# Opening stage of a two-layer block: modulation rows and the sum of squares moved to TensorE

## The chip, the cores and the metric

One core of one Trainium2 chip runs the whole kernel as one program. The metric is device time in microseconds (us), the median of several runs. Engines: TensorE (PE in the profile; PEld is its weight load), VectorE (DVE), ScalarE (ACT), GpSimd (POOL), SyncE (SP, which here only issues DMAs).

## The reference, cut to what matters

The whole is one block on T = 256 tokens of D = 1024 features (attention mixers, a feed-forward part, an expert lookup). The change touches only its first lines: the vector `c` makes six modulation vectors; the first two, shift and scale, act on the normalised input; the result goes into the wide input projection.

```python
def rmsnorm(x, g):
    return x * lax.rsqrt(jnp.mean(x * x, axis=-1) + 1e-6) * g

mod = silu(c) @ w_ada + b_ada              # 6*D values; shift = mod[:D], scale = mod[D:2*D], ...
h = rmsnorm(x, norm1_g) * (1 + scale) + shift
z = h @ w_in                               # w_in: D x 5704, cut into tiles of 128 columns
```

## The kernel before, in words

Features lie on the partitions: `x` is 8 feature tiles of 128 features by 256 tokens. All products keep fp32 accuracy by a split into a high and a low part of a rounded type (fp32r): a product is three matmuls, high by high, high by low, low by high. A weight tile (128 x 1024, 512 KB) is loaded by SyncE into `wraw`, ScalarE rounds it to the high part (L98), and DVE or GpSimd subtracts to get the low part (L100).

The opening stage (`first_mixer`) does this:

- SyncE loads `c` as a row and `x` in four pairs of feature tiles. PE spreads `c` over 128 partitions (L251), ScalarE makes `cond` = silu(c) of it.
- ScalarE squares `x` in pairs (L303); DVE adds the pairs down to one tile (L305 to L307); one fp32 matmul with a matrix of ones sums it over the partitions (L314). DVE takes the mean (L326) and the reciprocal root (L172 to L174, with ScalarE's logarithm and exponential between) into `rstd`.
- `xr` = `x` * `rstd`: the first pair of feature tiles on DVE, the other three pairs on GpSimd (L336).
- For each feature tile k two rows of `w_ada` are needed, row 8+k (scale) and row k (shift). A row is a tile of 128 x 1024 values, loaded by SyncE into one of four buffers (two for even k, two for odd k), and DVE multiplies it by `cond` and sums along each partition in one instruction (L266), which gives one column of `mod`. Then DVE adds `b_ada` (L270), makes `gs` (L389), ScalarE makes the normalised tile `hn` high (L393) and `y`, and DVE the low part of `hn` (L395).
- PE multiplies the `hn` tiles by nine block tiles of `w_in` (256 columns for each matmul, L361 and L363) and by four tiles for the value projection (512 columns). A matmul is issued when both its feature tile and its weight tile are known.

The order of all this is written out by hand in the string `ORDER`: "a" takes the next feature tile (rows, `mod`, `gs`, `hn`, and the matmuls with the weight tiles there so far), "w" the next block tile, "v" the next tile of the value projection. `LOWS` says for each of the 13 weight tiles whether DVE ("v") or GpSimd ("g") makes the low part. All engines work through their own instructions in program order. The first matmul of the step after the stage is that of L469.

Of the kernel before, what the change touches and what calls it, by code (L numbers as in the profile page):

```python
# [9 lines left out]
FT = mybir.dt.float32  # L10
# [3 lines left out]
AF = mybir.ActivationFunctionType  # L14
OP = mybir.AluOpType
# [4 lines left out]
T = 256  # L20
D = 1024
KT = 8
EPS = 1e-6
NEG = -3.0e38
TAKEN = -3.4e38
ORDER = "wwawaavavwwawavwwaawv"
LOWS = "vgvgvgvvvvvgv"
EXP_LN = 6
SILU = 18
PLAN = "ijjaavaasvqvqvksskkssksqssrgrqsssrgss0gr1rggr0rrrgrg1rg20g31rg2rrg3rrgg23rg"  # L30
# [40 lines left out]
class Net:  # L71
# [171 lines left out]
    def load_cond(self, pool):  # L243

        nc = self.nc
        row = pool.tile([1, D], FT, name="crow")
        nc.sync.dma_start(row, self.ap["c"])
        self.cond = pool.tile([128, D], FT, name="cond")
        pss = [self.ps([128, 512], "mm") for _ in range(2)]
        for z, ps in enumerate(pss):  # L250
            nc.tensor.matmul(ps, self.ones[0:1, :], row[:, 512 * z:512 * z + 512], start=True, stop=True)  # L251

        def finish():
            for z, ps in enumerate(pss):
                self.last_act = nc.scalar.activation(self.cond[:, 512 * z:512 * z + 512], ps, AF.Silu)
            self.condd = self.dram.tile([1, D], FT, name="condd")
            nc.scalar.dma_start(self.condd, self.cond[0:1, :])
        return finish
# [25 lines left out]
    def first_mixer(self):  # L284
        nc, tc, ap = self.nc, self.tc, self.ap
        with ExitStack() as es:
            x1 = es.enter_context(tc.tile_pool(name="x1", bufs=1, side="right"))
            x = self.x = x1.tile([128, KT, T], FT, name="x")
            P = es.enter_context(tc.tile_pool(name="m1", bufs=1))
            A = es.enter_context(tc.tile_pool(name="m1a", bufs=1))  # L290
# [5 lines left out]
            nc.vector.tensor_scalar(self.upper, self.relx[:, 128:], 0.0, None, op0=OP.is_gt)  # L296
            self.table = self.act_table(SILU)
            cond = self.load_cond(A)
            sq = P.tile([128, KT, T], FT, name="sqs", tag="bias1")
            for k in range(0, KT, 2):  # L300
                nc.sync.dma_start(x[:, k:k + 2], ap["x"][:, k:k + 2])
                with tc.issue_after(self.table):
                    high = nc.scalar.activation(sq[:, k:k + 2], x[:, k:k + 2], AF.Square)  # L303
                if k % 4:
                    nc.vector.tensor_add(sq[:, k - 2:k], sq[:, k - 2:k], sq[:, k:k + 2])  # L305
            nc.vector.tensor_add(sq[:, :2], sq[:, :2], sq[:, 4:6])
            pair = nc.vector.tensor_add(sq[:, 0], sq[:, 0], sq[:, 1])  # L307
            with tc.issue_after(high.ins):
                cond()
            self.table = self.act_table(EXP_LN, self.last_act)  # L310
            nc.scalar.dma_start(self.vecs, self.ap["vecs"])
            nc.scalar.dma_start(self.b_ada, self.ap["b_ada"])
            ps = self.ps([128, T], "sm")
            nc.tensor.matmul(ps, self.ones, sq[:, 0], start=True, stop=True)  # L314
            r = P.tile([128, T], FT, name="rstd")
            n1 = Scratch(P.tile([128, 3 * T], FT, name="norm1", tag="kx"))
            ms = n1.tile([128, T], FT, name="ms")
            rows = [Scratch(P.tile([128, 2 * D], FT, name=f"ada{i}", tag=t)) for i, t in enumerate(("sgb", "bias1"))]

            def ada_row(k, j):  # L320
                self.ada_one(A, j, rows[k % 2].tile([128, D], FT, name="ada", bufs=2))

            with tc.issue_after(pair.ins):
                ada_row(0, 8)
            with tc.issue_after(self.last_ada.ins):
                mean = nc.vector.tensor_scalar(ms, ps, 1.0 / D, EPS, op0=OP.mult, op1=OP.add)  # L326
            with tc.issue_after(mean.ins):
                ada_row(0, 0)
            with tc.issue_after(self.last_ada.ins):
                self.rsqrt(n1, r, ms, [128, T])  # L330
            norm_exp = self.last_exp
            bg = P.tile([128, KT], FT, name="bg")
            nc.vector.scalar_tensor_tensor(bg, self.b_ada[:, 8:16], 1.0, self.vecs[:, 0], op0=OP.add, op1=OP.mult)
            xr = P.tile([128, KT, T], FT, name="xr", tag="sga")
            for k in range(0, KT, 2):
                (nc.gpsimd if k else nc.vector).tensor_tensor(  # L336
                    xr[:, k:k + 2], x[:, k:k + 2], r[:, None, :].to_broadcast([128, 2, T]), op=OP.mult)

            hn = self.hi_lo("hn0")
            qi = P.tile([128, 4, T], FT, name="qi", tag="qx")  # L340
# [3 lines left out]
            first, parts, lows, heads = [], [], [], {}  # L344
            known = 0
            F = tc.tile_pool(name="m1f", bufs=1)
            f = F.__enter__()
# [4 lines left out]
            spare += [[f.tile([128, D], FR, name=f"w0{i}{j}") for j in range(2)] for i in range(3)]  # L352
            banks = [self.ps([128, 2, T], t) for t in ("acc", "acc", "mm", "mm", "sm")]
            vacc = [self.ps([128, 512], "acc") for _ in range(2)]
            nlow = iter(LOWS)

            def product(bank, out, l, r, last):

# [6 lines left out]
            def block_part(i, k, a, b):  # L365
                o = slice(k * 128, k * 128 + 128)
                product(i // 2, banks[i // 2][:, i % 2], first[i][a][:, o], hn[b][:, k], a == 1 and k == KT - 1)

            def v_part(c, a, b):
                for k in (2 * c, 2 * c + 1):  # L370
                    for tb in range(2):
                        product(8 + tb, vacc[tb], hn[b][:, k, tb * 128:tb * 128 + 128],
                                parts[c][a][:, (k % 2) * 512:(k % 2) * 512 + 512], a == 1 and k == KT - 1)

            def later(part, *a):
                lows.append(lambda: part(*a))

            def flush():
                while lows:
                    lows.pop(0)()  # L380

            for e in ORDER:
                if e == "a":
                    k = known
                    if k:
                        ada_row(k, 8 + k)
                        ada_row(k, k)
                    self.ada_end(k, k + 1)
                    nc.vector.scalar_tensor_tensor(self.gs[:, 0, k:k + 1], self.mod[:, 8 + k:9 + k],  # L389
                                                   self.vecs[:, 0, k:k + 1], bg[:, k:k + 1], op0=OP.mult, op1=OP.add)  # L390
                    y = P.tile([128, T], FT, name="y1", bufs=2)
                    for t in (hn[0][:, k], y):
                        nc.scalar.activation(t, xr[:, k], AF.Identity, scale=self.gs[:, 0, k:k + 1],  # L393
                                             bias=self.mod[:, k:k + 1])
                    nc.vector.tensor_tensor(hn[1][:, k], y, hn[0][:, k].bitcast(FT), op=OP.subtract)  # L395
                    flush()
                    for b in range(2):
                        for i in range(len(first)):
                            block_part(i, k, 0, b)
                    for i in range(len(first)):  # L400
                        block_part(i, k, 1, 0)
                    known += 1
                    continue
                c = len(parts)
                with tc.issue_after(norm_exp.ins), tc.issue_after(self.last_rsqrt.ins):
                    w = self.weights(ap["w_in"][len(first) if e == "w" else 9 + c], next(nlow),
                                     spare.pop() if e == "w" else None)
                if e == "w":
                    i = len(first)
                    first.append(w)  # L410
                    flush()
                    for k in range(known):
                        block_part(i, k, 0, 0)
                        block_part(i, k, 0, 1)
                        later(block_part, i, k, 1, 0)
                else:
                    parts.append(w)
                    flush()
                    v_part(c, 0, 0)
                    v_part(c, 0, 1)  # L420
                    later(v_part, c, 1, 0)
# [4 lines left out]
            ps = banks[4][:, 0]  # L426
# [40 lines left out]
            ps = self.ps([128, 2, 8], "sm")  # L467
# [4 lines left out]
            with tc.issue_after(qi_last.ins):  # L472
# [4 lines left out]
                ps = self.ps([128, 384], "sm")  # L477
# [5 lines left out]
                rows = self.dram.tile([128, 8 * 384], FT, name="rows")[:, :]  # L483
                nc.scalar.dma_start(rows, bass.AP(tensor=line.tensor, offset=line.offset, ap=[[0, 128], [1, 8 * 384]]))
                bias = []
                for tb in range(2):
# [3 lines left out]
                                                   ap=[[8 * 384 - 1, 128], [384, 8], [1, n]]))  # L490
# [70 lines left out]
            for j2 in range(4):  # L561
                wa = self.weights(ap["w_proj"][2 * j2])
                wb = self.weights(ap["w_proj"][2 * j2 + 1])
                for i in range(2):
                    j = 2 * j2 + i
                    pa = self.fm_block(wa, ya, 4, i * 512, self.ps([128, T], "acc"))
                    m = W.tile([128, T], FT, name="m")
# [16 lines left out]
            for j in range(8):  # L584
                ps = self.fm_block(self.weights(ap["w_out"][j]), mg)
                nc.vector.scalar_tensor_tensor(x[:, j], ps, self.mod[:, 16 + j:17 + j], x[:, j],
                                               op0=OP.mult, op1=OP.add)
# [851 lines left out]
def _col(v):  # L1439
    return v.reshape(-1, 128).T  # L1440
# [10 lines left out]
def prepare(inputs):  # L1451
    i = {k: np.asarray(v) for k, v in inputs.items()}
    ar = np.arange
    o = {}
    o["x"] = i["x"][0].T.reshape(8, 128, 256).transpose(1, 0, 2)
    o["mem"] = i["mem_2"][0].T.reshape(8, 128, 256).transpose(1, 0, 2)
    o["c"] = i["c"]
    o["w_ada"] = i["w_ada"][0].T.reshape(48, 128, 1024)
    o["b_ada"] = _col(i["b_ada"][0])
    o["vecs"] = np.stack([_col(v) for v in (  # L1460
        i["norm1_g"][0], i["norm2_g"][0], i["final_g"], i["norm_mix_g_2"][0], i["norm_xattn_g_2"][0],
        i["norm_mem_g_2"][0], i["norm_ffn_g_2"][0])], axis=1)
    w = i["w_in"][0]
# [14 lines left out]
    w = i["w_in_2"][0]  # L1478
# [39 lines left out]
```

## Time and profile before

| what | us |
|---|---|
| median of 3 runs (lowest, highest) | 1450.46 (1448.54, 1452.81) |
| the profiled execution's own time | 1451.56 |
| its span in the profile | 1449.8 |
| PE busy in the span | 1382.8 (95%) |
| DVE busy | 1102.9 (76%) |
| ACT busy | 756.3 (52%) |
| POOL busy | 151.3 (10%) |

The span is what the profile shows; the time of the execution holds 1.76 us more around it. A row of a timeline reads: start and length in us, engine, line of the kernel, operation, written tile <- read tiles, shape, count of instructions put together, and in brackets how long the engine had been idle and what ended that.

### The profile page before, as it was taken

Reading aid. Unit: us, or ns where it says so; the run is one execution under the profiler, and the core shown is the slowest. Engines: PE = TensorE matmul, PEld = TensorE weight load, DVE = VectorE, ACT = ScalarE, POOL = GpSimd, SP = SyncE. Lnnn points to the kernel's source line nnn. Section 1 sums busy time; section 2 is a strip of 40 time slices with the busy share of each in tenths; the row PEclk is TensorE's granted clock in tenths of the full one; section 3 lists DMA queues with packets and bytes.
Section 4 is the critical chain, followed back from the end, with each engine's and each line's share of the span. In section 5 each row is a group of like instructions: output and inputs, shape, how many; then the busy total and the mean of one; then the engine's idle time right before and its main releaser. Section 6 shows DMA issues by size and latency. Waiting matters only on the chain. (4 is left out here: it accounts for less than half of the span.)

```text
span 1449.8 us, 28871 instructions
## 1 busy us (share of the span) xinstructions
PE 1382.8 (95%) x11584; PEld 1326.8 (92%) x11584; DVE 1102.9 (76%) x2082; ACT 756.3 (52%) x1358; POOL 151.3 (10%) x64
## 2 busy tenths in 40 slices
PE   4989899999898999999999999999999999899997
PEld 2879799899898999999999999999999879799996
DVE  7797988549999888999856556665557796777776
ACT  4546664455445555555554444444445465655555
POOL 3100000018995000000000000000000000000001
PEclk9999999999999999999999999999999999999998
DMA  7766776655555545545566666776664444266662
GB/s 278 268 202 230 267 243 200 207 186 156 169 186 161 168 153 166 166 151 171 152 207 221 198 189 192 240 233 201 186 188 141 148 123 157 74 189 191 192 193 94
DMA packets 76234, 269.51 MB, mean 186 GB/s; under 512 B 8970, under 2 KB 11202, under 8 KB 75460
## 3 DMA queue, kind: packets, MB, share of 16 engines
q1 hardware_dynamic: 71426, 257.99, 55.6%
q10 hardware_dynamic: 4674, 9.69, 2.0%
q8 instruction: 90, 1.47, 0.4%
q14 instruction: 44, 0.36, 0.1%
HBM read 265.01 MB, written 4.21 MB: 186 GB/s over the span
## 5 line engine op out<-in xcount | busy, mean ns | idle before, releaser
L98 ACT ACTIVATE wh<-wraw 128x1024 fp32r<-128x1024 f32 x431 | 456.3, 1061 | 522.8 <-PE ps_acc L130 244.1
L100 DVE TENSOR_TENSOR wl<-wraw,wh 128x1024 fp32r<-128x1024 f32 x384 | 470.3, 1227 | 253.9 <-ACT wh L98 251.1
L129 PE MATMUL ps_acc<-c,wh 128*128 128x256 f32 x1024 | 286.6, 280 | 0.0
L130 PE MATMUL ps_acc<-c,wh 128*128 128x256 f32 x1024 | 286.5, 280 | 0.0
L131 PE MATMUL ps_acc<-c,wl 128*128 128x256 f32 x1024 | 286.5, 280 | 0.0
L131 PE MATMUL ps_mm<-hn,wl 128*128 128x256 f32 x680 | 190.1, 280 | 9.8 <-DVE wl L100 7.1
L131 PE MATMUL ps_acc<-hn,wl 128*128 128x256 f32 x696 | 192.5, 277 | 4.7 <-POOL wl L100 4.7
L129 PE MATMUL ps_mm<-hn,wh 128*128 128x256 f32 x680 | 192.6, 283 | 2.7 <-ACT wh L98 2.6
L129 PE MATMUL ps_acc<-hn,wh 128*128 128x256 f32 x696 | 193.9, 280 | 0.0
L129 PEld LDWEIGHTS ps_acc<-c,wh 128*128 128x128 f32 x1024 | 192.5, 188 | 0.1
L131 PEld LDWEIGHTS ps_acc<-c,wl 128*128 128x128 f32 x1024 | 192.5, 188 | 0.0
L130 PEld LDWEIGHTS ps_acc<-c,wh 128*128 128x128 f32 x1024 | 192.5, 188 | 0.0
L130 PE MATMUL ps_acc<-hn,wh 128*128 128x256 f32 x696 | 192.4, 277 | 0.0
L130 PE MATMUL ps_mm<-hn,wh 128*128 128x256 f32 x680 | 189.5, 279 | 0.0
L131 PEld LDWEIGHTS ps_mm<-hn,wl 128*128 128x128 f32 x680 | 128.2, 189 | 11.6 <-DVE wl L100 8.6
L100 POOL TENSOR_TENSOR wl<-wraw,wh 128x1024 fp32r<-128x1024 f32 x47 | 131.8, 2826 | 56.4 <-ACT wh L98 56.2
L131 PEld LDWEIGHTS ps_acc<-hn,wl 128*128 128x128 f32 x696 | 130.8, 188 | 5.4 <-POOL wl L100 5.4
L129 PEld LDWEIGHTS ps_mm<-hn,wh 128*128 128x128 f32 x680 | 128.9, 190 | 5.2 <-ACT wh L98 3.3
L130 PEld LDWEIGHTS ps_acc<-hn,wh 128*128 128x128 f32 x696 | 130.7, 188 | 0.2 <-DVE hn L281 0.2
L129 PEld LDWEIGHTS ps_acc<-hn,wh 128*128 128x128 f32 x696 | 130.4, 188 | 0.4 <-ACT hn L280 0.2
L130 PEld LDWEIGHTS ps_mm<-hn,wh 128*128 128x128 f32 x680 | 128.5, 189 | 0.2
L1404 POOL TENSOR_TENSOR big<-big 128x512 f32<-128x512 f32 x4 | 5.0, 1265 | 981.8 <-DVE big L1401 981.8
(484 smaller groups left out, 2770.9 us busy)
## 6 DMA issues: line engine op xcount, KB each, us to landing
wraw<-in_peer_u_dram SPq DMA_DIRECT2D x128, 512.0 KB, 4.0
wraw<-in_peer_v_dram SPq DMA_DIRECT2D x128, 512.0 KB, 4.4
wraw<-in_w_in_dram SPq DMA_DIRECT2D x70, 512.0 KB, 4.8
wraw<-in_ffn_up_dram SPq DMA_DIRECT2D x44, 512.0 KB, 3.6
wraw<-in_ffn_down_dram SPq DMA_DIRECT2D x22, 512.0 KB, 3.6
ada<-in_w_ada_dram SPq DMA_DIRECT2D x16, 512.0 KB, 6.0
wraw<-in_w_out_dram SPq DMA_DIRECT2D x16, 512.0 KB, 4.6
wraw<-in_peer_wq_dram SPq DMA_DIRECT2D x16, 512.0 KB, 3.6
```

Of the source, the lines that this page charges most:

```text
L98: nc.scalar.activation(h, raw, AF.Copy)
L100: (nc.vector if eng == "v" else nc.gpsimd).tensor_tensor(l, raw, h.bitcast(FT), op=OP.subtract)
L129: mm(out, a[0], b[0], start=first, stop=False, **kw)
L130: mm(out, a[0], b[1], start=False, stop=False, **kw)
L131: self.last_mm = mm(out, a[1], b[0], start=False, stop=last, **kw)
L1404: nc.gpsimd.tensor_tensor(xf[:, tb, cs], xt[:, tb, cs], fg[:, cs], op=OP.mult)
```

## The change: rows on TensorE, sum of squares on TensorE, another order

The two rows of each of the first `ADA_PE` = 4 feature tiles are no longer multiplied on DVE. Each row is stored transposed in blocks of 128, and PE multiplies its eight blocks (128 x 128, the stationary operand, fp32) by one column of `cond_col` each, eight matmuls summed into one column of `mods`. `cond_col` is silu of the new input `c_col`, `c` with features on the partitions. `mods` lies in the PSUM bank that takes the sum of squares. That sum is now eight matmuls with ones, one for each feature tile; the four adds on DVE are gone. GpSimd does nothing in the stage: all low parts and all pairs of `xr` are DVE's, and a pair of `xr` is made when the first of its tiles comes up. `crow` is loaded from ScalarE's queue, `ccol` is the first load on SyncE's. The string `ORDER` is another one. Feature tiles 4 to 7 keep their rows on DVE.

```diff
-ORDER = "wwawaavavwwawavwwaawv"
-LOWS = "vgvgvgvvvvvgv"
+ORDER = "awwawawawwvvaawwvwaav"
+ADA_PE = 4
...
-        nc.sync.dma_start(row, self.ap["c"])
+        nc.scalar.dma_start(row, self.ap["c"])
+        col = pool.tile([128, KT], FT, name="ccol")
+        nc.sync.dma_start(col, self.ap["c_col"])
+        self.cond_col = pool.tile([128, KT], FT, name="cond_col")
+        with self.tc.issue_after(self.table):
+            nc.scalar.activation(self.cond_col, col, AF.Silu)
...
+            ps = self.ps([128, 2 * T], "sm")
+            mods = ps[:, T:T + 16]
+            def ada_row(k, j):
+                w = rows[k % 2].tile([128, D], FT, name="ada", bufs=2)
+                if k >= ADA_PE:
+                    return self.ada_one(A, j, w)
+                self.load(w, self.ap["w_ada"][j])
+                for i in range(KT):
+                    with tc.issue_after(bank.ins):
+                        nc.tensor.matmul(mods[:, j:j + 1], w[:, i * 128:i * 128 + 128], self.cond_col[:, i:i + 1],
+                                         start=False, stop=i == KT - 1, skip_group_check=True)
...
-                if k % 4:
-                    nc.vector.tensor_add(sq[:, k - 2:k], sq[:, k - 2:k], sq[:, k:k + 2])
-            nc.vector.tensor_add(sq[:, :2], sq[:, :2], sq[:, 4:6])
-            pair = nc.vector.tensor_add(sq[:, 0], sq[:, 0], sq[:, 1])
+                for i in (k, k + 1):
+                    with tc.issue_after(bank.ins) if i else ExitStack():
+                        m = nc.tensor.matmul(ps[:, :T], self.ones, sq[:, i], start=i == 0, stop=i == KT - 1,
+                                             skip_group_check=True)
+                    bank = bank if i else m
...
-            nc.tensor.matmul(ps, self.ones, sq[:, 0], start=True, stop=True)
...
-            with tc.issue_after(pair.ins):
-                ada_row(0, 8)
-            with tc.issue_after(self.last_ada.ins):
-                mean = nc.vector.tensor_scalar(ms, ps, 1.0 / D, EPS, op0=OP.mult, op1=OP.add)
+            mean = nc.vector.tensor_scalar(ms, ps[:, :T], 1.0 / D, EPS, op0=OP.mult, op1=OP.add)
+            ada_row(0, 8)
+            ada_row(0, 0)
             with tc.issue_after(mean.ins):
-                ada_row(0, 0)
-            with tc.issue_after(self.last_ada.ins):
                 self.rsqrt(n1, r, ms, [128, T])
...
-            for k in range(0, KT, 2):
-                (nc.gpsimd if k else nc.vector).tensor_tensor(
-                    xr[:, k:k + 2], x[:, k:k + 2], r[:, None, :].to_broadcast([128, 2, T]), op=OP.mult)
+            def scaled(k):
+                nc.vector.tensor_tensor(xr[:, k:k + 2], x[:, k:k + 2], r[:, None, :].to_broadcast([128, 2, T]),
+                                        op=OP.mult)
...
-                    self.ada_end(k, k + 1)
-                    nc.vector.scalar_tensor_tensor(self.gs[:, 0, k:k + 1], self.mod[:, 8 + k:9 + k],
+                    if k % 2 == 0:
+                        scaled(k)
+                    on_pe = k < ADA_PE
+                    raw = mods if on_pe else self.mod
+                    nc.vector.tensor_add(self.mod[:, k:k + 1], raw[:, k:k + 1], self.b_ada[:, k:k + 1])
+                    nc.vector.scalar_tensor_tensor(self.gs[:, 0, k:k + 1], raw[:, 8 + k:9 + k],
```

On PE the stage began like this before: the spread of `c`, the one sum, then block matmuls of feature tile 0 with the first two weight tiles (`hn_153` is the high part of `hn`, `hn_154` the low part, `w_...` parts of block tiles).

```order
L251 MATMUL ps_mm<-crow,ones 128x512 x2
L314 MATMUL ps_sm<-sqs,ones 128x256
L363 MATMUL ps_acc<-hn_153,w_176 128x256
L361 MATMUL ps_acc<-hn_153,w_174 128x256
L363 MATMUL ps_acc<-hn_153,w_172 128x256
```

Now the start of PE's program reads so (`ada_112` is the buffer of feature tile 0's rows, `ada_113` that of tile 1's):

```order
L325 MATMUL ps_sm<-sqs,ones 128x256
L256 MATMUL ps_mm<-crow,ones 128x512 x2
L325 MATMUL ps_sm<-sqs,ones 128x256 x7
L315 MATMUL ps_sm<-cond_col,ada_112 128x1 x16
L315 MATMUL ps_sm<-cond_col,ada_113 128x1 x16
L374 MATMUL ps_acc<-hn_168,w_191 128x256
L372 MATMUL ps_acc<-hn_169,w_191 128x256
```

The four rows of tiles 0 and 1 stand ahead of the first block matmul. The rows of tile 2 stand further on in PE's program, with three block matmuls between them (high part of `hn`, three weight tiles):

```order
L315 MATMUL ps_sm<-cond_col,ada_112 128x1 x8
L372 MATMUL ps_acc<-hn_168,w_191 128x256
L372 MATMUL ps_acc<-hn_168,w_189 128x256
L372 MATMUL ps_acc<-hn_168,w_187 128x256
L315 MATMUL ps_sm<-cond_col,ada_112 128x1 x8
L372 MATMUL ps_acc<-hn_169,w_191 128x256
```

On DVE, before, tile 0's rows stood around the mean (`norm_131`) and the steps of the reciprocal root:

```order
L266 SCALAR_TENSOR_TENSOR junk,mod<-ada_132,cond 128x1024
L389 SCALAR_TENSOR_TENSOR gs<-mod,vecs,bg 128x1
L326 TENSOR_SCALAR norm_131<-ps_sm 128x256
L266 SCALAR_TENSOR_TENSOR junk,mod<-ada_132,cond 128x1024
L172 TENSOR_TENSOR norm_131<-norm_131 128x256
L270 TENSOR_TENSOR mod<-mod,b_ada 128x1
L173 SCALAR_TENSOR_TENSOR norm_131<-norm_131 128x256
L174 SCALAR_TENSOR_TENSOR rstd<-norm_131 128x256
L100 TENSOR_TENSOR w_177<-wraw,w_176 128x1024
L336 TENSOR_TENSOR xr<-x,rstd 128x512
```

Now the same place on DVE has no row; `mod` and `gs` read the PSUM bank, and the reciprocal root stands behind them:

```order
L337 TENSOR_SCALAR norm_140<-ps_sm 128x256
L403 TENSOR_TENSOR mod<-ps_sm,b_ada 128x1
L404 SCALAR_TENSOR_TENSOR gs<-ps_sm,vecs,bg 128x1
L172 TENSOR_TENSOR norm_140<-norm_140 128x256
L173 SCALAR_TENSOR_TENSOR norm_140<-norm_140 128x256
L174 SCALAR_TENSOR_TENSOR rstd<-norm_140 128x256
L100 TENSOR_TENSOR w_192<-wraw,w_191 128x1024
L348 TENSOR_TENSOR xr<-x,rstd 128x512
```

So DVE's chain to the first `xr` now waits for two rows on PE where it had two rows of its own.

## Rows read from the trace of the kernel before

**Rows 1.** The page, busy time of each engine, share of the span, instructions.

```profile
PE 1382.8 (95%) x11584; PEld 1326.8 (92%) x11584; DVE 1102.9 (76%) x2082; ACT 756.3 (52%) x1358; POOL 151.3 (10%) x64
```

**Rows 2.** Stretches: length, busy PE, PEld, DVE, ACT, POOL, PEclk, DMA share, GB/s.

```profile
10.00:20.00 10.00, 2.23 (x5) 1.22 (x5) 9.89 (x16) 5.30 (x8) 5.12 (x3) 1.00 0.96 363
20.00:30.00 10.00, 5.34 (x18) 4.26 (x18) 9.95 (x13) 2.04 (x3) 5.29 (x3) 1.00 0.45 138
...
34.80:68.70 33.90, 32.99 (x236) 30.63 (x234) 25.92 (x38) 19.40 (x28) 4.90 (x2) 1.00 0.78 281
```

**Rows 3.** Waits, 0 to 34.8 us: total, times, longest.

```profile
ACT hn L393 <- DVE mod L270: 12.3, 3, 7.3
```

**Rows 4.** Timeline: marks of the stage, on ACT and PE.

```profile
17.64 0.60 ACT L393 ACTIVATE hn<-xr,mod,gs 128x256 fp32r<-128x256 f32 x1 [1.50 <-DVE xr L336]
18.29 0.58 PE L363 MATMUL ps_acc<-hn,w 128*128 128x256 f32 x1 [6.35 <-ACT hn L393]
...
34.18 0.60 ACT L393 ACTIVATE hn<-xr,mod,gs 128x256 fp32r<-128x256 f32 x1 [1.97 <-DVE mod L270]
...
68.72 0.29 PE L469 MATMUL ps_sm<-ident,wiT 8*128 8x8 f32 x2
```

**Rows 5.** Groups by line and form, 0 to 70 us: busy, mean ns, idle before.

```profile
L266 DVE SCALAR_TENSOR_TENSOR junk<-ada,cond 128x1024 f32<-128x1024 f32 x16 | 21.7, 1354 | 0.1
...
L305 DVE TENSOR_TENSOR sqs<-sqs 128x512 f32<-128x512 f32 x2 | 1.4, 693 | 3.1 <-ACT sqs L303 3.1
```

**Rows 6.** Timeline, 14 to 33 us: DVE, and one GpSimd instruction.

```profile
14.72 1.22 DVE L100 TENSOR_TENSOR w<-wraw,w 128x1024 fp32r<-128x1024 f32 x1
15.86 1.75 DVE L336 TENSOR_TENSOR xr<-x,rstd 128x512 f32<-128x512 f32 x1
...
20.90 2.53 POOL L100 TENSOR_TENSOR w<-wraw,w 128x1024 fp32r<-128x1024 f32 x1
21.14 3.37 DVE L266 SCALAR_TENSOR_TENSOR junk<-ada,cond 128x1024 f32<-128x1024 f32 x1
...
28.64 2.32 DVE L389 SCALAR_TENSOR_TENSOR gs<-mod,vecs,bg 128x1 f32<-128x1 f32 x1
...
32.59 0.21 DVE L389 SCALAR_TENSOR_TENSOR gs<-mod,vecs,bg 128x1 f32<-128x1 f32 x1
```

**Rows 7.** Timeline of PE: block matmuls of 256 columns.

```profile
18.67 0.41 PE L361 MATMUL ps_acc<-hn,w 128*128 128x256 f32 x1
18.89 0.41 PE L363 MATMUL ps_acc<-hn,w 128*128 128x256 f32 x1
...
31.78 1.01 PE L361 MATMUL ps_acc<-hn,w 128*128 128x256 f32 x3 [1.22 <-ACT hn L393]
...
58.31 0.52 PE L361 MATMUL ps_acc<-hn,w 128*128 128x256 f32 x3
```

**Rows 8.** PE with narrow matmuls: timeline, durations (lowest, median, highest ns), stretches.

```profile
195.41 1.40 PE L188 MATMUL ps_sm<-ones,sq 128*128 128x1 f32 x12
...
1100.26 2.06 PE L188 MATMUL ps_sm<-big 128*128 128x2 f32 x9
...
L188 PE MATMUL ps_sm<-big x11: 251/352/352, 1100.0 to 1102.0; 128*128 128x2 f32 x11
...
195.41:196.81 1.40, 1.40 (x15) 1.40 (x14) 1.40 (x4) 1.27 (x3) 0.00 (x0) 1.00 0.80 269
1100.20:1102.10 1.90, 1.90 (x11) 1.90 (x10) 1.44 (x2) 0.32 (x1) 0.00 (x0) 0.50 0.85 246
```

**Rows 9.** Timeline, 0 to 12 us: the spread of `c`, a Square, the mean.

```profile
2.49 3.75 PE L251 MATMUL ps_mm<-crow,ones 1*128 1x512 f32 x4 [2.49 <-DMA crow<-in_c_dram]
4.11 0.63 ACT L303 ACTIVATE sqs<-x 128x512 f32<-128x512 f32 x1 [2.10 <-DMA x<-in_x_dram]
...
11.98 0.42 DVE L326 TENSOR_SCALAR norm<-ps_sm 128x256 f32<-128x256 f32 x1
...
L251 PE MATMUL ps_mm<-crow,ones 1*128 1x512 f32 x4 | 3.7, 1089 | 2.5 <-DMA crow<-in_c_dram 2.5
```

**Rows 10.** The page, DMA issues of the rows: KB each, us to landing.

```profile
ada<-in_w_ada_dram SPq DMA_DIRECT2D x16, 512.0 KB, 6.0
```

More of the change, by code (lines that the diff above doesn't have):

```diff
@@ L298, in first_mixer @@
             cond = self.load_cond(A)
-            sq = P.tile([128, KT, T], FT, name="sqs", tag="bias1")
+            rows = [Scratch(P.tile([128, 2 * D], FT, name=f"ada{i}", tag=t)) for i, t in enumerate(("sgb", "bias1"))]
+            ps = self.ps([128, 2 * T], "sm")
[9 more added lines that the diff above has]
+                                         start=False, stop=i == KT - 1, skip_group_check=True)
+            sq = P.tile([128, KT, T], FT, name="sqs", tag="hm1")
             for k in range(0, KT, 2):
@@ L303, in first_mixer @@
                     high = nc.scalar.activation(sq[:, k:k + 2], x[:, k:k + 2], AF.Square)
-                if k % 4:
-                    nc.vector.tensor_add(sq[:, k - 2:k], sq[:, k - 2:k], sq[:, k:k + 2])
-            nc.vector.tensor_add(sq[:, :2], sq[:, :2], sq[:, 4:6])
-            pair = nc.vector.tensor_add(sq[:, 0], sq[:, 0], sq[:, 1])
-            with tc.issue_after(high.ins):
-                cond()
+                for i in (k, k + 1):
[3 more added lines that the diff above has]
+                    bank = bank if i else m
+                if k == 4:
+                    with tc.issue_after(high.ins):
+                        cond()
             self.table = self.act_table(EXP_LN, self.last_act)
@@ L312, in first_mixer @@
             nc.scalar.dma_start(self.b_ada, self.ap["b_ada"])
-            ps = self.ps([128, T], "sm")
-            nc.tensor.matmul(ps, self.ones, sq[:, 0], start=True, stop=True)
             r = P.tile([128, T], FT, name="rstd")
@@ L317, in first_mixer @@
             ms = n1.tile([128, T], FT, name="ms")
-            rows = [Scratch(P.tile([128, 2 * D], FT, name=f"ada{i}", tag=t)) for i, t in enumerate(("sgb", "bias1"))]
-            def ada_row(k, j):
-                self.ada_one(A, j, rows[k % 2].tile([128, D], FT, name="ada", bufs=2))
-            with tc.issue_after(pair.ins):
-                ada_row(0, 8)
-            with tc.issue_after(self.last_ada.ins):
-                mean = nc.vector.tensor_scalar(ms, ps, 1.0 / D, EPS, op0=OP.mult, op1=OP.add)
+            mean = nc.vector.tensor_scalar(ms, ps[:, :T], 1.0 / D, EPS, op0=OP.mult, op1=OP.add)
+            ada_row(0, 8)
+            ada_row(0, 0)
             with tc.issue_after(mean.ins):
-                ada_row(0, 0)
-            with tc.issue_after(self.last_ada.ins):
                 self.rsqrt(n1, r, ms, [128, T])
@@ L354, in first_mixer @@
             vacc = [self.ps([128, 512], "acc") for _ in range(2)]
-            nlow = iter(LOWS)
             def product(bank, out, l, r, last):
@@ L405, in first_mixer @@
                 with tc.issue_after(norm_exp.ins), tc.issue_after(self.last_rsqrt.ins):
-                    w = self.weights(ap["w_in"][len(first) if e == "w" else 9 + c], next(nlow),
+                    w = self.weights(ap["w_in"][len(first) if e == "w" else 9 + c], "v",
                                      spare.pop() if e == "w" else None)
@@ L1457, in prepare @@
     o["c"] = i["c"]
+    o["c_col"] = _col(i["c"][0])
     o["w_ada"] = i["w_ada"][0].T.reshape(48, 128, 1024)
+    pe = [j + k for j in (0, 8) for k in range(ADA_PE)]
+    o["w_ada"][pe] = o["w_ada"][pe].reshape(-1, 128, 8, 128).transpose(0, 3, 2, 1).reshape(-1, 128, 1024)
     o["b_ada"] = _col(i["b_ada"][0])
```

## The prediction

> **What bounds the kernel now.** I read the totals first: TensorE (PE) is busy for 95% of the span [rows 1], so a time lost or won in the opening lasts to the end unless PE later stands still for other reasons. The table by stretch says where PE is not the limit [rows 2]: between 10 and 30 us it works 7.6 us of 20 while VectorE (DVE) works 19.8. From 34.8 to 68.7 PE is busy 32.99 of 33.90 us. Up to 34.8 us the opening is therefore bound by whatever makes the normalised feature tiles, behind that by PE. The waits say the same: ScalarE's `hn` waits 12.3 us for `mod` on DVE [rows 3], and PE for `hn`. So the mark that carries the result is when the fourth feature tile's `hn` is there: 34.18 + 0.60 = 34.78 us [rows 4]. Behind it stand 33.9 us of PE work up to the first matmul of L469, at 68.72 [rows 4].
>
> Why DVE is late: a modulation row costs it 1.354 us on average, 16 of them 21.7 us [rows 5], and while GpSimd runs its low part (20.90 to 23.43) a row beside it takes 3.37 us; `gs`, 0.21 at 32.59, takes 2.32 at 28.64 [rows 6].
>
> **The clock.** The opening runs at TensorE's lower level, 1.2 GHz, though the column of granted clock reads 1.00 (no change is recorded before 35 us): the matmuls of 256 columns follow each other at 18.67 and 18.89, 0.22 us apart, and from 58.31 three of them take 0.52 with 0.28 for the last, 0.12 apart [rows 7]. It rises near 35 us, when PE has worked without a gap since 31.78 [rows 7]. It can fall under narrow matmuls: in the midst of a run of two-column ones, from 1100.2, the grant is 0.50 (1.2 GHz) [rows 8].
>
> **Part by part.** All times below are us from the start of the span.
>
> *Sum of squares.* Before, one matmul behind DVE's adds; its DVE successor (`mean`) begins at 11.98 [rows 9]. Now PE does eight fp32 matmuls of 256 columns. The `crow` product shows four 512-column instructions in 3.75 us, of 1.09 each on average [rows 9]; where the ends overlap, the spacing is (3.75 − 1.09)/3 = 0.89. That is 0.44 for 256 columns, and an fp32 matmul is two instructions (the two of `crow` are listed as x4 [rows 9]): 0.89 a matmul. PE can begin when the first Square ends, 4.11 + 0.63 = 4.74 [rows 9], and does 4 × 0.89 = 3.6 of `crow` and 8 × 0.89 = 7.1 of sums: 15.4 if the clock stays low, some 13 if it rises near 10, as it did near 35 under gapless work. I take 14.0. `mean` (0.42) ends at 14.4; this is 2 us later than before, though four DVE adds are gone.
>
> *Tile 0's two rows.* Each is 8 matmuls of 128x128 weights and one column, 16 instructions. They wait for `mean`, since they write the bank it reads. Here the price hangs on the clock. Twelve instructions of one column take 1.40 us at 195.41, where the grant is 1.00: 0.117 each at most, (1.40 − 0.25)/11 = 0.105 if the last one has 0.25 to drain. At 0.50, nine of two columns take 2.06: 0.229 at most, (2.06 − 0.35)/8 = 0.214 with 0.35 to drain. 0.25 and 0.35 are what such an instruction shows at either level [rows 8]. A row is 1.7 or 3.4 us, against 1.36 on DVE. For tile 0, just behind the sums, I take the clock as still up: 3.4 for both, done at 18.2 (low: 6.8).
>
> The Trainium skill (TensorE: Matmul & The Clock Gate, section LDWEIGHTS) puts a weight load at columns/1.2 in ns, 107 ns for 128, without regard to the array's clock. Here the row at 1.00 agrees, that at 0.50 (0.214 us) does not; by the rule alone every row would cost 1.7, which is the first rival below.
>
> *DVE behind it:* `mod` and `gs`, 0.21 each, three steps of the reciprocal root (each like the 0.42 of `mean` [rows 9]), the weight's low part 1.22, `xr` 0.69 (the size of a wide add, without GpSimd beside it) [rows 5, 6], then `hn` 0.60 on ScalarE: 18.2 + 0.4 + 1.3 + 1.22 + 0.69 + 0.6 = 22.4. Tile 0's `hn` ended at 18.24 before [rows 4].
>
> *Tile 1's rows stand on PE ahead of the first block matmul,* as the order shows, and wait for `gs` of tile 0, 18.2 + 0.4 = 18.6. PE has done only one-column work since 14 and the clock is low by then: 2 × 3.4 → 25.4. There the first block matmul starts, at 18.29 before [rows 4]. Eight block matmuls at 0.21 and a wait of about 1 for the low part: 28.0.
>
> *Rows of tiles 2 and 3* lie between block matmuls: row 3.4 (31.4), three matmuls 0.6 (32.0), row 3.4 (35.4), 22 matmuls 4.7 (40.1), row (43.5), three (44.1), row (47.5), then `mod`, `gs` and `hn`, 1.0: the fourth tile is there at 48.5, against 34.78: 13.7 late.
>
> *The loads* of tile 2's rows wait for PE to free tile 0's buffers (about 18.2), and weight tiles are queued behind them on SyncE. A row's load takes 6.0 us [rows 10], so they land near 25; PE wants them at 28. I add nothing; low bound nothing, high bound 2 where two queue up.
>
> *The rest of the stage.* Before: 33.9. Now, 216 matmuls of 256 columns and 48 of 512 in the stage, less the 36 small ones done: 180 × 0.12 + 48 × 0.24 = 33.1, and the first 2 us of it at half rate cost 1 more: 34.1. 48.5 + 34.1 = 82.6 against 68.72: +13.9. If the clock rises within the 22 matmuls ahead of tile 3's rows, these cost 1.7 each: +10.5. I take +13, nearer the first: before, the clock rose near 35 under gapless block matmuls [rows 7], and here narrow rows stand on both sides of those 22.
>
> *What DVE saves:* eight rows (10.8), four adds (693 ns for the wide ones [rows 5]) and the slowed instructions beside GpSimd; it takes on four low parts of 1.22 and three `xr` of 0.69. That is all on an engine that, by the above, waits for PE's rows; I cost the saving at nothing, since PE's rows up to 48 us hide it. It is worth up to what is worked out in the third rival.
>
> The shift stays: past 68.7 PE is the bound in the 95% of rows 1. On the profiled execution's own 1451.56: 1464.6; the median of the runs is 1.1 below that execution, so **1463.5**.
>
> **Rivals.**
> 1. *One-column matmuls cost at 1.2 GHz what they cost at 2.4.* Six rows of tiles 1 to 3 then save 1.7 each, 10.4: +3.5, 1454. For: the instruction is mostly a weight load. Against: 0.214 at 0.50 beside 0.105 [rows 8]; though those have two columns. Chance 0.09.
> 2. *The clock rises during the sums and stays up through the rows.* Then besides the rows the block matmuls are at full rate, tile four comes near 35 and the stage ends at 67 to 69: 1450, no change. Against: it fell amid narrow work [rows 8]. Chance 0.06.
> 3. *The other side: DVE is the bound and its relief arrives.* Beside GpSimd three of its instructions alone lose 5.2 us (3.37 for 1.35, 2.32 for 0.21, 1.75 for 0.69 [rows 5, 6]), and the balance of work moved is 10.8 + 2.5 − 4.9 − 2.1 = 6.3: 11.5, of which I would expect two thirds to reach the end, 7.5: 1443. It decides if the fourth `hn` comes before 34.8. From 14.4 to there PE has 20 us; the eight rows alone cost 27 at the low clock, 14 at the high one, and they stand in the chain rather than beside it. Chance 0.08. The Trainium skill (SBUF — State Buffer, section Who interferes with whom) has a DVE instruction with two SBUF inputs blocked by a GpSimd instruction that reads SBUF; the 3.37 us beside GpSimd's 2.53 agree.
> 4. *Worse:* the sums stay at the low clock (+1.4), tile 0's rows too (+3.4), and loads queue up (+2): +17 to +20, 1467 to 1470. Chance 0.07.
>
> The forecast itself, +10 to +15 (1460 to 1466), has 0.70.
>
> **How the numbers follow.** 0.3% of the time, 4.35 us, is about what a measurement of this kernel can tell from no change: 1446.1 to 1454.8. Faster is the third rival and a third of the second: 0.10. The same is the first rival, rather more than half of it at that edge, and the rest of the second: 0.12. Slower, 0.78. The range goes from just below the first rival, 1453.5, to the middle of the fourth, 1469; it leaves out rivals two and three and a part of the fourth, 0.18. The likeliest case's own range is 1460 to 1466.
>
> **What would show it.** Right: instructions of one column 0.2 us apart from about 18 us; the first block matmul near 25; the fourth `hn` at 45 to 50; PE's rows at L315 some 25 us in all; the first matmul of the L469 step (L484 now) at 79 to 84; GpSimd idle and no DVE instruction on a row over 1.4 us. Wrong: rows of 1.7 us each (first or second rival, told apart by the spacing of block matmuls beside them), or a fourth `hn` near 30 with PE still waiting on DVE (third), or the shift at 68.7 made up later, where PE waits for transfers that an earlier start would not have hastened.

## The result and the profile after

The changed kernel takes 1466.84 us (median of 4 runs, 1466.16 to 1467.08), the kernel before 1451.63 in the same series: ratio 1.0100, 95% interval 1.0087 to 1.0113. It is slower by some 15 us; 1463.5 was forecast, in a range from 1453.5 to 1469. The likeliest case, 1460 to 1466, is passed by 0.8 us.

The page of the changed kernel, its span and the first engines (busy us, share, instructions):

```profile
span 1465.2 us, 29131 instructions
PE 1410.0 (96%) x11726; PEld 1356.2 (93%) x11726; DVE 1087.3 (74%) x2069; ACT 756.2 (52%) x1359; POOL 135.0 (9%) x57
```

PE is 27 us longer at work than before [rows 1] in a span that is 15.4 longer: the narrow matmuls keep it busy, but they also keep `hn` waiting. The timeline of the stage in the changed kernel, the marks that the prediction named:

```profile
9.97 4.96 PE L325 MATMUL ps_sm<-sqs,ones 128*128 128x256 f32 x14
...
14.97 0.42 DVE L337 TENSOR_SCALAR norm<-ps_sm 128x256 f32<-128x256 f32 x1 [1.90 <-PE ps_sm L325]
...
15.45 3.73 PE L315 MATMUL ps_sm<-cond_col,ada 128*128 128x1 f32 x32 [0.52 <-DVE norm L337]
...
19.56 6.42 PE L315 MATMUL ps_sm<-cond_col,ada 128*128 128x1 f32 x32 [0.38 <-DVE gs L404]
...
22.52 0.60 ACT L408 ACTIVATE hn<-xr,mod,gs 128x256 fp32r<-128x256 f32 x1 [4.34 <-DVE xr L348]
...
25.83 0.56 PE L374 MATMUL ps_acc<-hn,w 128*128 128x256 f32 x1
...
28.22 3.41 PE L315 MATMUL ps_sm<-cond_col,ada 128*128 128x1 f32 x16
...
32.27 3.41 PE L315 MATMUL ps_sm<-cond_col,ada 128*128 128x1 f32 x16
...
40.38 1.99 PE L315 MATMUL ps_sm<-cond_col,ada 128*128 128x1 f32 x16
...
42.67 2.09 PE L315 MATMUL ps_sm<-cond_col,ada 128*128 128x1 f32 x16
...
45.12 0.60 ACT L408 ACTIVATE hn<-xr,mod,gs 128x256 fp32r<-128x256 f32 x1 [7.04 <-DVE gs L404]
...
80.62 0.28 PE L484 MATMUL ps_sm<-ident,wiT 8*128 8x8 f32 x2
```

Where the first `hn` began at 17.64 and the fourth at 34.18 [rows 4], they now begin at 22.52 and 45.12. The first block matmul starts at 25.83 instead of 18.29, the step behind the stage at 80.62 instead of 68.72. The same 16 instructions take 3.41 us in one place and 1.99 in another; the stretches of the changed kernel say why (columns as in [rows 2]; the third from the end is the granted clock):

```profile
15.40:20.20 4.80, 4.38 (x38) 4.29 (x38) 0.95 (x4) 2.73 (x4) 0.00 (x0) 1.00 0.43 147
20.30:40.60 20.30, 20.14 (x94) 19.84 (x95) 9.09 (x16) 5.17 (x8) 0.00 (x0) 0.50 0.54 184
40.80:44.00 3.20, 3.20 (x30) 3.20 (x30) 0.00 (x0) 0.00 (x0) 0.00 (x0) 1.00 0.93 365
44.20:50.80 6.60, 5.59 (x26) 5.48 (x27) 4.31 (x7) 4.89 (x6) 0.00 (x0) 0.50 0.70 245
51.00:80.60 29.60, 29.60 (x206) 27.32 (x205) 20.96 (x36) 14.20 (x23) 0.00 (x0) 1.00 0.71 254
...
102.20:105.40 3.20, 3.20 (x16) 3.20 (x17) 3.17 (x6) 0.42 (x1) 0.00 (x0) 0.50 1.01 285
```

From 20.3 to 40.6 us PE is busy for 20.14 of 20.30 us, but at 1.2 GHz, and DVE works 9 us of 20, where it worked all the time before [rows 2]. The bound has gone over from DVE to PE. The waits of the changed kernel up to 84 us (total, times, longest) say the same:

```profile
DVE mod L403 <- PE ps_sm L315: 18.7, 4, 7.0
```

DVE, for which `hn` waited 12.3 us before [rows 3], now itself waits 18.7 us for the rows on PE. Its own eight rows cost 1219 ns each with GpSimd idle, not 1354 [rows 5]:

```profile
L271 DVE SCALAR_TENSOR_TENSOR junk<-ada,cond 128x1024 f32<-128x1024 f32 x8 | 9.8, 1219 | 0.1
```

### The profile page after: what moved, and what is told of

Read it like the earlier page. It is cut to its first block, busy times and chain, and to the rows that moved or that the text cites. A ratio compares the mean times of both kernels' runs of the same rounds, so it can differ in the third digit from the quotient of the medians.

```text
span 1465.2 us, 29131 instructions
## 1 busy us (share of the span) xinstructions
PE 1410.0 (96%) x11726; PEld 1356.2 (93%) x11726; DVE 1087.3 (74%) x2069; ACT 756.2 (52%) x1359; POOL 135.0 (9%) x57
## 5 line engine op out<-in xcount | busy, mean ns | idle before, releaser
L100 DVE TENSOR_TENSOR wl<-wraw,wh 128x1024 fp32r<-128x1024 f32 x385 | 469.8, 1223 | 253.8 <-ACT wh L98 251.5
L131 PEld LDWEIGHTS ps_mm<-hn,wl 128*128 128x128 f32 x680 | 129.2, 190 | 13.6 <-DVE wl L100 10.6
L100 POOL TENSOR_TENSOR wl<-wraw,wh 128x1024 fp32r<-128x1024 f32 x46 | 129.0, 2826 | 50.5 <-ACT wh L98 50.3
```

Source lines behind the costliest of these rows:

```text
L100: (nc.vector if eng == "v" else nc.gpsimd).tensor_tensor(l, raw, h.bitcast(FT), op=OP.subtract)
L131: self.last_mm = mm(out, a[1], b[0], start=False, stop=last, **kw)
```

## The experiments

All ratios are to the kernel before in the same series, whose medians were 1451.6 to 1454.0; they are recorded with their intervals and can differ a little from the quotient of the two medians.

| variant | median us | ratio | 95% interval |
|---|---|---|---|
| changed kernel | 1466.84 | 1.0100 | 1.0087 to 1.0113 |
| changed, rows back on DVE | 1455.52 | 1.0007 | 0.9991 to 1.0022 |
| changed, order of before | 1461.02 | 1.0046 | 1.0029 to 1.0063 |
| before, nothing on GpSimd | 1443.81 | 0.9927 | 0.9907 to 0.9947 |
| changed, half of each row | 1459.13 | 1.0031 | 1.0019 to 1.0044 |
| before, nothing on GpSimd, new order | 1451.14 | 0.9990 | 0.9978 to 1.0001 |
| before, nothing on GpSimd, sums on PE | 1443.51 | 0.9943 | 0.9926 to 0.9959 |
| before, nothing on GpSimd, rows of tile 1 on PE | 1444.87 | 0.9949 | 0.9933 to 0.9966 |
| changed, rows 32 columns wide | 1471.14 | 1.0131 | 1.0109 to 1.0153 |
| changed, last "w" later | 1464.38 | 1.0077 | 1.0053 to 1.0100 |
| before, nothing on GpSimd, new order, last "w" later | 1446.58 | 0.9953 | 0.9938 to 0.9968 |
| before, low parts on DVE | 1449.04 | 0.9976 | 0.9960 to 0.9993 |
| before, nothing on GpSimd, sums on PE, new order, last "w" later | 1445.49 | 0.9951 | 0.9936 to 0.9965 |

The theory: the rows on TensorE, mostly at its lower clock and in the chain to `hn`, are the loss. The rivals: the new order, the sums, or the work taken over from GpSimd.

**Rows back on DVE.**

```diff
-ADA_PE = 4
+ADA_PE = 0
```

> The changed kernel with no row on TensorE: all sixteen on VectorE again; new order, sum of squares on TensorE and an idle GpSimd stay. Theory (the rows on TensorE, mostly at its lower clock and ahead of the block matmuls, are the whole loss): the loss goes; VectorE can do the rows of tiles 0 and 1 while it waits for the sums (mean at 14.97 us in the changed kernel), so the fourth feature tile comes by 30 to 36 us and the time is 1448 to 1456, at most 4 us above the kernel before. Rival (the other order, or the sum of squares on TensorE, or the work taken over from GpSimd is to blame): 1461 or more.

1.0007: the loss goes with the rows, 0.0093 of 1453, 13.5 us. In its profile the stage ends at 67.95, 12.7 us before that of the changed kernel. But it also shows that all the rest of the change together gives no gain, though GpSimd is idle in it.

**Order of before.**

```diff
-ORDER = "awwawawawwvvaawwvwaav"
+ORDER = "wwawaavavwwawavwwaawv"
```

> The changed kernel with the order string of before: two weight tiles ahead of the first further feature tile, rows of tiles 0 to 3 still on TensorE. Theory: the same 128 one-column matmuls, about 20 us of them at the lower clock, are on the path; 1460 to 1469, within 6 us of the changed kernel. Rival (the new order makes the loss by putting the rows ahead of the block matmuls): at or near the kernel before, 1448 to 1456.

1461.02 lies in the theory's range, near its lower end: the rows remain a loss with the old order, but 0.0054, some 8 us, belongs to the order. In its profile the stage ends at 80.66, as in the changed kernel (80.62): what the order costs here lies behind the stage (the table below).

**Nothing on GpSimd, in the kernel before.**

```diff
-LOWS = "vgvgvgvvvvvgv"
+LOWS = "vvvvvvvvvvvvv"
...
-            for k in range(0, KT, 2):
-                (nc.gpsimd if k else nc.vector).tensor_tensor(
-                    xr[:, k:k + 2], x[:, k:k + 2], r[:, None, :].to_broadcast([128, 2, T]), op=OP.mult)
+            def scaled(k):
+                nc.vector.tensor_tensor(xr[:, k:k + 2], x[:, k:k + 2], r[:, None, :].to_broadcast([128, 2, T]),
+                                        op=OP.mult)
...
+                    if k % 2 == 0:
+                        scaled(k)
                     self.ada_end(k, k + 1)
```

> The kernel before with GpSimd's part of the stage on VectorE: all low parts, and the pairs of the scaled input, each made when its first tile comes up. VectorE takes on four low parts of 1.22 us and three pairs of 0.69, 7.0 us in all, of which about 4 stand before the fourth feature tile, and is rid of at least 5.2 us lost beside GpSimd. Theory (GpSimd's removal is near nothing): 1447 to 1454. Rival (the relief is a large gain that the rows on TensorE hide): 1440 to 1446. Rival (the work moved to VectorE is a large part of the loss): 1456 or more.

0.9927: the rival of a large gain was right. This is the lowest ratio of all; 0.9943 with the sums on PE, below, can't be told from it. Its stretches (columns as in [rows 2]):

```profile
20.00:30.00 10.00, 8.69 (x36) 7.36 (x36) 10.00 (x25) 4.24 (x7) 0.00 (x0) 1.00 0.85 300
30.00:62.00 32.00, 31.43 (x227) 29.05 (x225) 25.62 (x41) 18.83 (x28) 0.00 (x0) 1.00 0.81 313
```

DVE has no more time than before, but in the 10 us to 30 it gets 25 instructions through, where it got 13 [rows 2], and PE works 8.69 us instead of 5.34. The same instructions are shorter on DVE: up to 70 us its rows take 1218 ns each instead of 1354, `gs` 214 instead of 479, the low part of `hn` 420 instead of 558. The fourth `hn` ends in it at 30.44, and the stage at 62 instead of 68.7:

```profile
29.86 0.58 ACT L396 ACTIVATE hn<-xr,mod,gs 128x256 fp32r<-128x256 f32 x1
```

**Half of each row.** Line L315's loop:

```diff
-                for i in range(KT):
+                for i in range(KT // 2):
```

> The changed kernel with four of the eight matmuls of each row on TensorE; the other half of each row's sum is left out. Loads, waits and order stay. Theory: the one-column matmuls are on the path at 0.11 us an instruction for tile 0, 0.21 for tiles 1 and 2, and between them for tile 3: half of 3.7 + 6.4 + 6.8 + 4.1 = 21 us goes, 10.5, and the time is 1455 to 1459. Rival (the loads of the rows, or VectorE, set the pace, and the matmuls only fill a wait): 1464 to 1467.

1.0031, 10.0 us below the changed kernel (0.0069 of 1453), for half of 21 us of matmuls; 1459.13 us is at the upper edge of what was expected. The row matmuls are on the path nearly one to one, and the loads, which are as before, are not.

**New order without rows on PE, and sums without the new order** (both on top of the variant with nothing on GpSimd; the first changes the line `ORDER` alone, the second makes `sq` eight tiles to the end and sums them on PE as the change does).

```diff
...
-            nc.vector.tensor_add(sq[:, :2], sq[:, :2], sq[:, 4:6])
-            pair = nc.vector.tensor_add(sq[:, 0], sq[:, 0], sq[:, 1])
+                for i in (k, k + 1):
+                    with tc.issue_after(bank.ins) if i else ExitStack():
+                        m = nc.tensor.matmul(ps, self.ones, sq[:, i], start=i == 0, stop=i == KT - 1,
+                                             skip_group_check=True)
+                    bank = bank if i else m
```

> The kernel before with GpSimd's part on VectorE (1443.8 us in the run before this) and the new order string; rows and sum of squares as before. The variant with no row on TensorE, which has this order and the sums on TensorE, took 1455.5. Theory (the order is most of these 11.7 us: it leaves VectorE behind after the stage): 1449 to 1455. Rival (the sums on TensorE, which bring the mean 3 us later, are most of it): 1442 to 1447.

> The kernel before with GpSimd's part on VectorE, the old order, and the eight sum matmuls on TensorE in place of four adds and one matmul. The mean came at 15 us with such sums, against 12.2 in the variant without. Theory (the order is most of the 11.7 us): 1443 to 1448, since VectorE fills the wait with rows. Rival (the sums are most of it): 1450 to 1456.

0.9990 and 0.9943 against 0.9927: the order costs some 9 us where no row is on PE, as expected; the sums can't be told from nothing.

**Rows of tile 1 alone on PE** (on top of the variant with nothing on GpSimd; `mods` in a half bank of its own).

```diff
...
+            last = self.ps([128, 2, T], "sm")
+            mods = last[:, 1, :16]
...
-                self.ada_one(A, j, rows[k % 2].tile([128, D], FT, name="ada", bufs=2))
+                w = rows[k % 2].tile([128, D], FT, name="ada", bufs=2)
+                if k not in ADA_PE:
+                    return self.ada_one(A, j, w)
```

> The kernel before with GpSimd's part on VectorE, and only the two rows of feature tile 1 on TensorE, in half a bank that nothing else uses yet, so that they wait for no mean and no other row. TensorE is idle from 12.1 to 18.5 us there. If rows on TensorE are bad for their place in the chain alone, this is free and spares VectorE 2 x 1.3 us: 1440 to 1443. If their time at the lower clock (2 x 3.4 us) pushes the block matmuls or the next tile: 1445 or more.

1444.87 falls between the two ranges, and 0.9949 is no gain over 0.9927. Its timeline of PE says that the idle place wasn't there to be had:

```profile
17.77 3.54 PE L337 MATMUL ps_sm<-cond_col,ada 128*128 128x1 f32 x16 [5.77 <-DMA ada<-in_w_ada_dram]
21.17 0.56 PE L382 MATMUL ps_acc<-hn,w 128*128 128x256 f32 x1
...
21.96 3.41 PE L337 MATMUL ps_sm<-cond_col,ada 128*128 128x1 f32 x16
```

The first row waits for its load until 17.77, the second stands behind three block matmuls, and tile 1's `mod` comes at 25.40 us, where DVE's own rows gave it at 21.68 in the variant with nothing on GpSimd.

**Rows of 32 equal columns.**

```diff
-            mods = ps[:, T:T + 16]
+            mods = ps[:, T:].rearrange("p (j n) -> p j n", n=32)
...
-                        nc.tensor.matmul(mods[:, j:j + 1], w[:, i * 128:i * 128 + 128], self.cond_col[:, i:i + 1],
+                        nc.tensor.matmul(mods[:, j % 8 + j // 8 * 4], w[:, i * 128:i * 128 + 128],
+                                         self.cond_col[:, i:i + 1].to_broadcast([128, 32]),
```

> The changed kernel, each row matmul with 32 columns that all hold the same value, of which one is read. If an instruction takes as long as its weight load, 0.11 us at the full clock and 0.21 at half, the 32 columns cost nothing by themselves. Theory (half of the rows' price is the lower clock, and this depends on what TensorE does): if the clock stays up, rows of tiles 1 and 2 take 1.8 us each, 6 us less in all, 1459 to 1463. Rival (the clock is as before): 1465 to 1468. If the columns cost: over 1469.

1.0131, 1471.14 us: by its time this is the third case, columns that cost. The trace says otherwise; in its timeline and stretches, one row of tile 3 and the clock:

```profile
41.14 3.46 PE L315 MATMUL ps_sm<-cond_col,ada 128*128 128x32 f32 x16
...
18.40:55.70 37.30, 36.29 (x167) 35.57 (x167) 14.19 (x26) 10.45 (x15) 0.00 (x0) 0.50 0.57 197
```

32 columns take 3.46 us for 16 instructions at 0.50, one column 3.41 (tile 2's rows above): 31 columns more cost nearly nothing. That the weight load is the price instead is likely, as PEld is busy for 35.57 of those 37.30 us, but no run varies it. This variant is slower by its clock: the grant is 0.50 from 18.4 to 55.7, and tile 3's rows cost 3.46 each instead of 2.0; its stage ends 5.1 us later, at 85.68. Why the clock stayed low for longer is not shown.

**The last "w" of the order later**, in the changed kernel and in the variant with nothing on GpSimd and the new order.

```diff
-ORDER = "awwawawawwvvaawwvwaav"
+ORDER = "awwawawawwvvaawwvaawv"
```

> The changed kernel with one letter of the order moved: the last block tile behind the last two feature tiles (...wvaawv in place of ...wvwaav), as in the order of before. Theory (what the order costs lies behind the stage: with the last two letters as they are, the copies of the block products come together at the end, and VectorE's next low part of a weight tile stands behind one more accumulation and a top-k): the stage ends as late, near 80 us, the next step is 4 to 5 us shorter, 1459 to 1463, like the changed kernel with the whole order of before (1461.0). Rival (the order costs inside the stage): 1465 to 1468.

> The kernel before with GpSimd's part on VectorE and the new order with the same letter moved. With the old order 1443.8, with the new one 1451.1. Theory of the tail: 1441 to 1445. Rival (the head of the new order, in which the first feature tile comes ahead of the weight tiles, is what costs): 1449 to 1452.

Without rows on PE the letter gives back 0.0037 (intervals apart), 5 of the 9 us that the order cost. 1446.58 lies between the two ranges expected, nearer the theory's. In the changed kernel its time is unsettled, 1460.4 to 1467.9 in six runs, between the two ranges in the median, with an interval that overlaps that of the changed kernel. In its profile the stage ended 2.3 us later (82.90), for tile 0's rows took 4.95 us there instead of 3.73 and tile 1's 6.99 instead of 6.42; these stand in PE's program ahead of the letter. What the letter does is seen in the timelines: the step behind the stage begins with a small transpose on PE, and PE waits for the low part of a weight tile in it. The changed kernel, the new order without rows on PE, and that with the letter moved:

```profile
96.59 0.39 PE L131 MATMUL ps_mm<-hn,wl 128*128 128x256 f32 x1 [2.86 <-DVE wl L100]
```

```profile
64.20 0.28 PE L472 MATMUL ps_sm<-ident,wiT 8*128 8x8 f32 x2
...
80.17 0.58 PE L131 MATMUL ps_mm<-hn,wl 128*128 128x256 f32 x1 [2.86 <-DVE wl L100]
```

```profile
63.56 0.28 PE L472 MATMUL ps_sm<-ident,wiT 8*128 8x8 f32 x2
...
78.34 0.39 PE L131 MATMUL ps_mm<-hn,wl 128*128 128x256 f32 x1 [1.12 <-DVE wl L100]
```

From the transpose to the end of this wait: 15.97 us in both kernels with the new order, 14.78 with the letter moved. In the program of the changed kernel two steps of the next token block (`L522`) and the last add of the first block's top-k (`L531`) stand on DVE between `L530` and that low part (rows of its order, from that place):

```
L530 TENSOR_SCALAR acc_689<-acc_689 128x128
L522 SCALAR_TENSOR_TENSOR acc_690<-rel,wi,acc_690 128x256
L531 TENSOR_TENSOR acc_689<-acc_689,cm 128x128
L522 SCALAR_TENSOR_TENSOR acc_690<-rel,wi,acc_690 128x256
L100 TENSOR_TENSOR wl<-wraw,wh 128x1024
```

With the letter moved `L100` stands right behind `L530`. After the longer wait the granted clock falls for some 3 us (in the changed kernel from 102.2, the last stretch shown of it, after two more waits of 1.42 and 0.76; in the new order without rows on PE from 80.3, here); in the variant with the letter moved it stays at 1.00:

```profile
80.30:83.40 3.10, 3.10 (x15) 3.10 (x16) 1.40 (x3) 0.60 (x1) 0.00 (x0) 0.50 0.97 260
```

```profile
78.00:90.00 12.00, 10.15 (x75) 8.99 (x76) 11.08 (x23) 5.91 (x9) 0.00 (x0) 1.00 0.98 334
```

What the letter is worth can be read from the step as a whole, from the transpose to a row of four small matmuls of `ka` and `qa` some 25 us on. That row in the changed kernel, the same with the letter moved, and in the kernel before:

```profile
107.73 0.49 PE L624 MATMUL ps_acc<-ka,qa 64*128 64x128 f32 x4 [0.43 <-ACT qa L461]
```

```profile
105.46 0.49 PE L624 MATMUL ps_acc<-ka,qa 64*128 64x128 f32 x4 [0.43 <-ACT qa L461]
```

```profile
92.35 0.49 PE L609 MATMUL ps_acc<-ka,qa 64*128 64x128 f32 x4 [0.43 <-ACT qa L446]
```

| variant (one profile each) | stage ends | `ka`, `qa` row | between |
|---|---|---|---|
| before | 68.72 | 92.35 | 23.63 |
| changed kernel | 80.62 | 107.73 | 27.11 |
| changed, rows back on DVE | 67.95 | 96.67 | 28.72 |
| changed, order of before | 80.66 | 103.28 | 22.62 |
| changed, last "w" later | 82.90 | 105.46 | 22.56 |
| before, nothing on GpSimd | 62.24 | 85.95 | 23.71 |
| before, nothing on GpSimd, new order | 64.20 | 92.79 | 28.59 |
| before, nothing on GpSimd, new order, last "w" later | 63.56 | 86.60 | 23.04 |

The other six variants fall in line: 27.07 to 29.97 with the last "w" where the change has it, 22.57 to 23.17 with it later, as the order of before has it. In each of the five kernels with the early "w" the granted clock falls within this step, in none of the nine others. So the early letter costs the next step 4.6 us in the changed kernel and 5.6 without rows on PE, by the two pairs that differ in it alone. The difference holds both the longer waits and the low clock; they were not separated. In the whole time of the changed kernel the gain is not clear of the spread of its runs.

**Low parts on DVE, scaled input on GpSimd**, in the kernel before (the line `LOWS` alone).

> The kernel before with all low parts on VectorE, and the three pairs of the scaled input still on GpSimd (14.88 to 20.93 us). It divides the gain of 10 us: if the low parts beside VectorE's rows are the loss, most of it is here, 1444 to 1447; if the scaled input is, 1450 to 1454.

0.9976: a third of the gain; 1449.04 lies between the two cases, near the second. The other two thirds come with the scaled input, which the variant with nothing on GpSimd also makes pair by pair when it is needed; these two were not separated. The timeline of this run shows what GpSimd's three `xr` do to the DVE beside them, two low parts in 4.49, where two take 2.35 with nothing on GpSimd:

```profile
15.66 6.05 POOL L336 TENSOR_TENSOR xr<-x,rstd 128x512 f32<-128x512 f32 x3 [14.29 <-DVE rstd L174]
...
18.30 4.49 DVE L100 TENSOR_TENSOR w<-wraw,w 128x1024 fp32r<-128x1024 f32 x2
```

**All that was free or better together.**

> All parts that the runs so far show free or better together: GpSimd's part on VectorE, the sums on TensorE, rows on VectorE, the new order with the last block tile later. If the parts add up: 1440 to 1445. If the sums cost in the new head (4.4 us between 1451.1 and 1455.5, where the rows of tile 1 also stood ahead of the first normalised tile): 1445 to 1449.

0.9951, 1445.49 us: the lower edge of the second case, and not better than nothing on GpSimd alone (0.9927, with the order of before). That variant, 0.9907 to 0.9947, beats both kernels. Against the same variant without the sums on PE (0.9953) the sums again can't be told from nothing.

## Why the prediction was right, and where it was not

The parts, each added to the last, in us of 1453 from the ratios: GpSimd's work to DVE −10.6; the new order +9.2; the sums, with the other way of loading `c`, +2.5 (the two intervals overlap); the rows +13.5. Sum +14.5. The intervals leave some 3 us open in each. The same parts at the end of the stage, by the profiles: −6.5, +2.0, +3.7, +12.7, together the +11.9 by which it ends later.

- **What bounds.** Right. DVE held `hn` up before; with GpSimd idle alone, the fourth tile comes 4.3 us earlier and the stage ends some 6.5 earlier. With the rows on PE, PE's rows bound it.
- **Sums:** `mean` ends at 15.4, not 14.4, since PE reaches the other seven only at 9.97, behind `crow`, where the terms of the sum (4.74 + 0.89 + 3.6) give 9.2.
- **Tile 0's rows at the full clock:** 3.73 for 3.4. **Tile 1's at the low one, ahead of the first block matmul:** 6.42 for 6.8; that matmul at 25.83 for 25.4. **Tile 2's:** 3.41 each for 3.4. The 0.105 and 0.214 us of an instruction, taken from far rows, held: 3.73/32 = 0.117 and 3.41/16 = 0.213, each with the end of the last one in it. The first rival, one price at both clocks, is out; so is the second, for the grant is 0.50 from 20.3.
- **Tile 3's rows:** mis-sized. I took 3.4 each and gave 1.7 as the other bound; the grant was 1.00 from 40.8 to 44.0, and they took 1.99 and 2.09. So the fourth tile is there at 45.72, 10.9 late, not 13.7.
- **Rest of the stage:** 34.9 for 34.1, since the clock fell again from 44.2 to 50.8. The stage ends at 80.62, between the two sums given, +11.9.
- **Loads at nothing:** held; PE waits for none of the rows' loads in the stage.
- **DVE's saving at nothing:** held in this change, since DVE waits 18.7 us for PE; but the third rival had its parts wrong. It put the loss beside GpSimd at 5.2 us, from three instructions, and the work that DVE takes on at 7.0, so that GpSimd's part alone would have given nothing; it gave 10.6. That DVE is slowed beside GpSimd was right; with the rows on PE the relief met another bound.
- **"The shift stays":** this step failed. It was 11.9 at the end of the stage, 13.4 at the wait of 96.59 (83.19 before), and 15.4 at the `ka`, `qa` row (107.73 for 92.35). I priced the order string only by where rows and tiles stand inside the stage, and not what it does to DVE's program behind it. The next step takes 27.11 us for 23.63; with the letter alone moved it takes 22.56, with the order of before 22.62. So the 3.5 us left out are the order's, made in that step. Farther on the shift is not constant: 13.1 at a table load of ScalarE (746.12 for 733.00), 15.3 at a later one (1277.68 for 1262.35), 15.4 at the end. The clock falls at different places in the two kernels; which of its falls does this is not shown.

So the total came close in part by luck. The chain of the rows held. Against the sum of +13.9, tile 3's rows were 2.8 too dear, the rest of the stage 0.8 too cheap, and the next step, 3.5, was left out: two misses that nearly cancel. Without rows on PE the order ends the stage 2.0 us later (64.20 for 62.24) and makes the next step 4.9 longer, 6.8 of the 8.8 us between the two profiles; where the other 2 arise stays open.

## What to carry to other kernels

A change of several parts can hide a gain: here 10 us from an idle GpSimd lay under two losses, the rows and the order, and running each part alone showed it. Before work goes to an engine that looks idle, price it at that engine's clock in that place, and ask when its operands land: PE stood idle for 12 of the 20 us from 10 to 30 because it waited at the end of a chain, and its rows went into that chain. An order written out for one stage also sets what the next stage finds; read the first waits behind it, and compare the length of the next stage, not only where this one ends.

## What the runs showed of the hardware that was not expected

A matmul instruction with 128 x 128 fp32 weights took 0.213 us at the granted 0.50 with one column and 0.216 with 32 (3.41 and 3.46 for 16), and 0.117 at 1.00 with one column (3.73 for 32). Two low parts on DVE beside GpSimd's three `xr` took 4.49 us instead of 2.35, and GpSimd's took 2.0 each where DVE makes one in 0.68: handing DVE's work to GpSimd made both slower here than DVE alone.
